# Trunk layer on one core: plain weight halves first, their sums in the halves' own places, and modulation rows in groups of 256 columns with tiles of their own

## The chip, the core and the metric

The kernel runs on one core of a Trainium2 chip. The metric is the device time of one execution in microseconds (us). Before the change it is 1999.14 us, the median of 3 runs (1997.41 to 2001.65).

## The reference, cut to what matters

One layer over 1056 tokens (1024 of a prompt, 32 of a second request with a condition vector of its own), model width 1024, all in float32:

```python
x = layer_norm(x)                                     # shared input norm
mod = silu(c) @ w_ada + b_ada                         # (9, 1024) for each of the two requests
f = (silu(mod1(x) @ w1) * (mod1(x) @ w3)) @ w2        # first feed-forward, width 2816
x = layer_norm(alpha * x + 0.5 * g1 * f)
m = mixer(mod2(x))                                    # RG-LRU group and gated spatial group
x = layer_norm(alpha * x + g2 * m)
f = (silu(mod3(x) @ v1) * (mod3(x) @ v3)) @ v2        # second feed-forward
x = layer_norm(alpha * x + 0.5 * g3 * f)
```

`modk(x)` is `x * (1 + scale_k) + shift_k`, and `g_k` is `1 + gate_k`. The nine rows of `mod` (three of shift, scale and gate each) come from one vector-matrix product with `w_ada`, 1024 x 9216.

## The kernel before

Activations lie transposed: 128 features to a partition block, 8 blocks, the tokens along the free axis in three chunks of 384, 384 and 288 columns (`CH`). A float32 product is made of three float32r matmuls: every operand is split into a high and a low part, and high*high, high*low and low*high are added in PSUM (`h_mm`, `p_mm`, `f_mm`, all through `mm`, L149). The split (`split`, L207 on ScalarE for the high part, L208 for the low one on VectorE, or on GpSimd where the caller says so) is made on the chip for weights and activations alike.

A feed-forward goes over 22 tiles of 128 hidden columns, in blocks of two (`BLOCKS`; the first and the last have three). For a tile, the H step makes the two products with `w1` and `w3`; for a block, the F step multiplies its gated tiles with `w2` and adds them into the residual (`add_gated`, L946 on VectorE).

From tile 3 on, the H step is `H_fast`: the two weight matrices are the rows of a 2 x 2 matrix of blocks (A11, A12 from `w1`, A21, A22 from `w3`, each 128 x 512 in memory, "halves" here), and the first two token chunks are the columns of another (B); seven products replace eight, in the manner of Strassen and Winograd. They need four sums of weight halves, S1 = A21 + A22, S2 = S1 - A11, S3 = A11 - A21, S4 = A12 - S2, made on GpSimd in `w_source` (L238, L239, L241, L243), and four sums of activation blocks, T1 to T4, made once for a feed-forward in `combs` and `comb_last` on VectorE (L789, L790). The third token chunk is multiplied in the plain way with the plain halves ("the sides"). PSUM has 8 banks, taken in turn by `ps`.

The order on TensorE is the order in which the code is written. A tile's eight weight halves are split in the order `PARTS` = A11, S2, A12, S1, S3, A22, S4, A21 into a ring of 8 tiles (`RING`) ahead of their use. Their raw form, 512 KB for `w1` and 512 KB for `w3` of a tile, is loaded by the SP queue (L202) into a ring of 5 tiles (`RAWS`), which also takes S1 and S2 (`wsum`) and the raw loads of `w_ada`. VectorE, ScalarE, GpSimd and SP get their order from a planner that simulates the program with times of its own; within an engine, instructions run strictly in that order, so one that waits holds up all behind it.

Two of the nine modulation rows are made at the start. The other seven (m = 2 to 8) are made during the first feed-forward by the generator `ada_rest`, which steps on as TensorE's planned time passes. For each half row of 512 columns it loads four tiles of 128 x 2 x 512 of `w_ada` (L698), accumulates 16 products with the condition vectors on VectorE (`acc`, L715 and L717), splits the sums, adds them over the partitions with four matmuls against a column of ones (`psm`), copies the two rows of the result to SBUF in two pieces (L732, into `s` tiles, the ring that the H step's intermediate results use too), writes them to DRAM (L733, on GpSimd's DMA queue), reads them back turned, so that the columns lie along partitions (L736, twice, same queue), and adds the bias on VectorE (`mod`, L738). Row 2, a gate, is needed by the first F step; the others later.

Of the kernel before, what the change touches and what calls it, by code (L numbers as in the profile page):

```python
# [12 lines left out]
F32 = mybir.dt.float32  # L13
# [38 lines left out]
PARTS = ["A11", "S2", "A12", "S1", "S3", "A22", "S4", "A21"]  # L52
RING, RAWS = 8, 5
# [68 lines left out]
class Core:  # L122
    def __init__(self, tc, ins, outs):
# [5 lines left out]
        self.n_s = 5  # L129
        self.ada_live = True  # L130
# [47 lines left out]
    def w_init(self):  # L178
        self.order = stream_order()
        self.raw_list = raw_order()  # L180
        self.raws = {}
        self.ws = {}
        self.sums = {}
        self.n_raw = self.n_split = self.n_rel = self.n_get = 0
        self.ring = [self.home(e) is None for e in self.order]
# [41 lines left out]
    def w_source(self, e):  # L227

        nm, t, h = e
# [4 lines left out]
        G = self.nc.gpsimd  # L234
        if h == "S2":
            x = self.wpool.tile([P, 1024], F32, tag="raw", name="wsum", bufs=RAWS)
            self.sums[nm, t] = x
            G.tensor_tensor(x[:, 0:512], a["A21"], a["A22"], ALU.add)  # L238
            G.tensor_tensor(x[:, 512:1024], x[:, 0:512], a["A11"], ALU.subtract)  # L239
        if h == "S3":  # L240
            G.tensor_tensor(a["A11"], a["A11"], a["A21"], ALU.subtract)  # L241
        if h == "S4":
            G.tensor_tensor(a["A12"], a["A12"], self.sums[nm, t][:, 512:1024], ALU.subtract)  # L243
        x = self.sums.get((nm, t))
        return {"S1": lambda: x[:, 0:512], "S2": lambda: x[:, 512:1024], "S3": lambda: a["A11"],
                "S4": lambda: a["A12"]}.get(h, lambda: a[h])()
# [25 lines left out]
    def w_rel(self, k=2):  # L272

        self.n_rel += k
        while self.n_split < len(self.order):
# [7 lines left out]
        need = {r for e in self.order[:n + 4] for r in raws_of(e)}  # L283
        open_ = {r for e in self.order[n:n + 16] for r in raws_of(e)} & set(self.raws)
        room = RAWS - self.ada_live - len(open_) - any(
            e[2] == "S4" and (e[0], e[1]) in self.sums for e in self.order[n:n + 8])
# [5 lines left out]
    def run(self):  # L292
# [51 lines left out]
        self.ffn(1, self.go(self.combs()), bg)  # L344
        self.drain(bg)
        self.ada_live = False
# [12 lines left out]
        self.n_s = 6  # L359
# [330 lines left out]
    def ada_rest(self):  # L690
# [4 lines left out]
        def raw(n):  # L695
            if n < 56 and n not in raws:
                r = self.wpool.tile([P, 2, 512], F32, tag="raw", name="raw", bufs=RAWS)
# [3 lines left out]
        raw(0)  # L701
        yield 1.0
        for m in (2, 3, 4, 5, 6, 7, 8):
            for h in range(2):
                acc = self.gpool.tile([P, 2, 512], F32, tag="acc", name="acc", bufs=1)
                for q in range(4):
                    n = ((m - 2) * 2 + h) * 4 + q
                    raw(n)
                    raw(n + 1)
                    r = raws.pop(n)  # L710
                    for kk in range(2):
                        k = 2 * q + kk
                        for v in range(2):
                            if k == 0:
                                V.tensor_scalar(acc[:, v, :], r[:, kk, :], self.cs[:, k, v:v + 1], None, ALU.mult)  # L715
                            else:
                                V.scalar_tensor_tensor(acc[:, v, :], r[:, kk, :], self.cs[:, k, v:v + 1],  # L717
                                                       acc[:, v, :], ALU.mult, ALU.add)
                    yield 2.5 if m == 2 else 7.0
                yield 5.0 if m == 2 else 9.0  # L720
                ps = self.ps("psm")
                for v in range(2):
                    t = [self.apool.tile([P, 512], F32R, tag="tot", name="acchl", bufs=self.ntot) for _ in range(2)]
                    self.split(t[0], t[1], acc[:, v, :])
# [862 lines left out]
```

## Time and profile before

| What | Value |
|---|---|
| median of 3 runs | 1999.14 us (1997.41 to 2001.65) |
| profiled execution | 2002.01 us, span 2000.3 us |
| mean granted TensorE clock | 0.971 |
| busy: TensorE, VectorE | 1876.9 us (94%), 1346.2 us (67%) |
| busy: ScalarE, GpSimd | 709.2 us (35%), 524.8 us (26%) |
| DMA | 140.16 MB, 70 GB/s mean |
| chain that ended last, largest share | TensorE 54% |

The stages in the span: start and the first H tile, with two modulation rows, to about 100 us; the rest of the first feed-forward to about 900 us, with the other seven rows until 773 us; the mixer to about 1300 us; the second feed-forward and the last norm to the end. The stage views give for each engine its busy time and, in brackets, its instructions; a matmul count in a stretch of equal kind of work is the measure of progress.

### The profile page before, as it was taken

How to read it: one execution, taken by the hardware profiler on the slowest of the kernel's cores; microseconds unless marked ns; L12 is line 12 of the kernel's file. 1: busy time of each engine (PE TensorE's matmuls, PEld its weight loads, DVE VectorE, ACT ScalarE, POOL GpSimd, SP SyncE). 2: the span in 40 equal slices, each digit the busy share in tenths (PEclk: the TensorE clock that was granted, in tenths of full speed). 3: DMA queues.
4: the chain of work that ended last, by engine and by line, in shares of the span. 5: the costliest groups of instructions: out<-in, count | busy, mean ns of one | idle time of the engine just before them, and what ended most of it. 6: DMA issues, size and time to landing. Idle time of an engine off the chain costs nothing.

```text
span 2000.3 us, 28452 instructions
## 1 busy us (share of the span) xinstructions
PE 1876.9 (94%) x11362; PEld 1819.9 (91%) x11362; DVE 1346.2 (67%) x2390; ACT 709.2 (35%) x1240; POOL 524.8 (26%) x428
## 2 busy tenths in 40 slices
PE   6979898899999898998999999999999999999996
PEld 3869898898998897998978999999999999999996
DVE  6889677687777685477397647695555545554567
ACT  5552222322322322325554434723222332223224
POOL 2213333333333433302200000023233323233310
PEclk8989899999999998999989999999999999999998
DMA  7331222222222220122201231001101111111102
GB/s 267 117 105 54 86 94 75 85 95 75 95 85 74 85 84 23 57 71 95 82 3 60 68 136 39 21 23 58 64 33 53 43 64 43 43 43 64 43 11 87
DMA packets 40949, 140.16 MB, mean 70 GB/s; under 512 B 6072, under 2 KB 8816, under 8 KB 40048
## 3 DMA queue, kind: packets, MB, share of 16 engines
q1 hardware_dynamic: 37104, 128.98, 18.9%
q10 hardware_dynamic: 1920, 9.24, 1.2%
q0 software_dynamic: 1792, 0.12, 0.4%
q8 instruction: 89, 1.46, 0.3%
q14 instruction: 44, 0.36, 0.1%
HBM read 129.53 MB, written 8.79 MB: 69 GB/s over the span
## 4 chain that ended last, share of the span: by engine, by line
PE 54%; DVE 5%; ACT 1%; issue 0%; POOL 0%; DMA 0%; POOLq 0%; DVEq 0%; ACTq 0%
PE ps L149 52%; PE psl L149 1%; PE psz L149 1%; DVE s L789 1%; PE psg L149 0%; DVE tot L952 0%; DVE xb L1065 0%; ACT t L543 0%; DVE t L1076 0%; DVE wh L208 0%; DVE xa L946 0%; DVE tx L208 0%; DVE xb L946 0%; ACT xh L550 0%; DVE s L790 0%
## 5 line engine op out<-in xcount | busy, mean ns | idle before, releaser
L149 PE MATMUL ps<-xh,wh 128*128 128x384 f32 (+1 forms) x3824 | 923.0, 324 | 45.1 <-DVE s L838 41.0
L149 PEld LDWEIGHTS ps<-xh,wh 128*128 128x128 f32 x3824 | 677.4, 192 | 55.6 <-DVE s L838 46.5
L149 PE MATMUL ps<-xl,wh 128*128 128x384 f32 (+1 forms) x1912 | 616.9, 323 | 3.3 <-DVE xl L553 3.2
L149 PE MATMUL ps<-g,wh 128*128 128x384 f32 (+1 forms) x2808 | 466.1, 325 | 13.0 <-DVE xa L946 4.7
L149 PEld LDWEIGHTS ps<-g,wh 128*128 128x128 f32 x2808 | 453.6, 189 | 19.6 <-DVE xa L946 6.7
L207 ACT ACTIVATE wh<-raw 128x512 fp32r<-128x512 f32 x376 | 234.7, 629 | 540.5 <-PE ps L149 517.1
L149 PEld LDWEIGHTS ps<-xl,wh 128*128 128x128 f32 x1912 | 367.4, 192 | 7.3 <-DVE xl L553 5.3
L208 DVE TENSOR_TENSOR wh<-raw,wh 128x512 fp32r<-128x512 f32 x283 | 207.2, 737 | 197.8 <-ACT wh L207 195.6
L208 POOL TENSOR_TENSOR wh<-raw,wh 128x512 fp32r<-128x512 f32 x93 | 129.3, 1392 | 417.0 <-ACT wh L207 416.9
L946 DVE SCALAR_TENSOR_TENSOR xb<-ps,gt,xb 128x384 f32<-128x384 f32 (+1 forms) x352 | 152.7, 488 | 102.6 <-PE ps L149 87.3
L717 DVE SCALAR_TENSOR_TENSOR acc<-raw,cs,acc 128x512 f32<-128x512 f32 x196 | 168.8, 897 | 6.5 <-DMA raw<-ada 6.3
L149 PE MATMUL ps<-tx,wh 128*128 128x384 f32 x912 | 167.3, 338 | 2.7 <-DVE s L838 2.6
L838 DVE TENSOR_TENSOR s<-s,ps 128x384 f32<-128x384 f32 x190 | 104.7, 551 | 87.4 <-PE ps L149 79.7
L149 PEld LDWEIGHTS ps<-tx,wh 128*128 128x128 f32 x912 | 158.9, 190 | 4.4 <-DVE s L838 3.6
L946 DVE SCALAR_TENSOR_TENSOR xa<-ps,gt,xa 128x384 f32<-128x384 f32 (+1 forms) x320 | 136.0, 481 | 23.5 <-PE ps L149 23.1
L208 POOL TENSOR_TENSOR wh<-wsum,wh 128x512 fp32r<-128x512 f32 x76 | 104.5, 1375 | 60.3 <-ACT wh L207 59.6
L207 ACT ACTIVATE g<-s 128x384 fp32r<-128x384 f32 (+1 forms) x126 | 62.4, 496 | 144.5 <-DVE s L679 144.0
L208 DVE TENSOR_TENSOR g<-s,g 128x384 fp32r<-128x384 f32 (+1 forms) x126 | 83.9, 666 | 39.4 <-ACT g L207 39.4
L238 POOL TENSOR_TENSOR wsum<-raw 128x512 f32<-128x512 f32 x38 | 57.8, 1522 | 142.4 <-DVE wh L208 86.0
L241 POOL TENSOR_TENSOR raw<-raw 128x512 f32<-128x512 f32 x38 | 53.3, 1403 | 148.1 <-DVE wh L208 101.5
L567 POOL TENSOR_TENSOR r<-r,half 128x3 f32<-128x3 f32 x8 | 7.4, 924 | 312.1 <-DVE r L566 312.1
L149 PE MATMUL ps<-T,wh 128*128 128x384 f32 x456 | 86.2, 337 | 0.0
(231 smaller groups left out, 1809.3 us busy)
## 6 DMA issues: line engine op xcount, KB each, us to landing
raw<-wst SPq DMA_DIRECT2D x156, 512.0 KB, 3.2
raw<-ada SPq DMA_DIRECT2D x64, 512.0 KB, 3.3
wnat<-ada SPq DMA_DIRECT2D x8, 512.0 KB, 9.9
xt<-x SPq DMA_DIRECT2D x7, 512.0 KB, 7.6
sp<-xa ACTq DMA_DIRECT2D x2, 1536.0 KB, 5.0
xb<-sp ACTq DMA_DIRECT2D x2, 1536.0 KB, 10.5
y<-xb SPq DMA_DIRECT2D x4, 768.0 KB, 3.2
sp<-xa ACTq DMA_DIRECT2D x1, 1152.0 KB, 4.1
```

The lines of the kernel that those rows point to most:

```text
L149: self.nc.tensor.matmul(out, a, b, start=start, stop=stop, skip_group_check=True)
L207: self.nc.scalar.activation(dst_h, src, AF.Copy)
L208: (e or self.nc.vector).tensor_tensor(dst_l, src, dst_h.bitcast(F32), ALU.subtract)
L238: G.tensor_tensor(x[:, 0:512], a["A21"], a["A22"], ALU.add)
L241: G.tensor_tensor(a["A11"], a["A11"], a["A21"], ALU.subtract)
L567: self.nc.gpsimd.tensor_tensor(out, out, self.half[:n, :w], ALU.pow)
L717: V.scalar_tensor_tensor(acc[:, v, :], r[:, kk, :], self.cs[:, k, v:v + 1], acc[:, v, :], ALU.mult, ALU.add)
L789: e.tensor_tensor(r, x[i][:, k, :].bitcast(F32), y[i][:, k, :].bitcast(F32), op)
L838: V.tensor_tensor(out, x, ps[:, :n], ALU.add)
L946: V.scalar_tensor_tensor(X[:, m, a + o:a + o + w], ps[:, o:o + w], self.gt[:, s, m, v:v + 1], X[:, m, a + o:a + o + w], ALU.mult, ALU.add)
```

## The change

Five things change.

- **Order of the halves.** `PARTS` becomes A11, A21, A12, A22, S2, S1, S3, S4, and `H_fast` is written in that order, with the sides put right behind the halves they use: A11, its side, A21's side, A12, its side, A22 (with T4), S2, S1, A22's side, S3, S4. The tile's last product is now S4's.
- **Sums in place.** A21 becomes S3, A22 becomes S2, A11 becomes S1 and A12 becomes S4, each in its own raw tile, with four GpSimd operations as before; `wsum` is gone. `RAWS` is 4, and raw tiles are asked for 12 halves ahead instead of 4 (4 in the first part of the mixer).
- **Modulation rows.** A unit is 256 columns: four loads of 128 x 2 x 256 (256 KB each), 32 accumulating operations of half the width for what took 16 before, and one row copy. Loads and row copies share a ring of their own, `ar`, of 2 tiles. The steps behind the sums (write, read back, bias) are written a step of the next unit's accumulation apart each, and the read-back and the bias come once for two units.
- **Activation sums of the first feed-forward.** T1 and T3 are made on GpSimd there (differences and low parts), with longer spacing; T2, T4 and the second feed-forward stay on VectorE.
- **F step.** With the block's last tile, the chunks 0, 2, 1 are taken over all of the group's output blocks instead of block by block. An `s` tile more (6) is there from the start.

```diff
-PARTS = ["A11", "S2", "A12", "S1", "S3", "A22", "S4", "A21"]
-RING, RAWS = 8, 5
+PARTS = ["A11", "A21", "A12", "A22", "S2", "S1", "S3", "S4"]
+RING, RAWS = 8, 4
...
-        if h == "S2":
-            x = self.wpool.tile([P, 1024], F32, tag="raw", name="wsum", bufs=RAWS)
-            self.sums[nm, t] = x
-            G.tensor_tensor(x[:, 0:512], a["A21"], a["A22"], ALU.add)
-            G.tensor_tensor(x[:, 512:1024], x[:, 0:512], a["A11"], ALU.subtract)
-        if h == "S3":
-            G.tensor_tensor(a["A11"], a["A11"], a["A21"], ALU.subtract)
-        if h == "S4":
-            G.tensor_tensor(a["A12"], a["A12"], self.sums[nm, t][:, 512:1024], ALU.subtract)
+        if h == "A22":
+            G.tensor_tensor(a["A21"], a["A11"], a["A21"], ALU.subtract)
+        if h == "S2":
+            G.tensor_tensor(a["A22"], a["A22"], a["A21"], ALU.subtract)
+            G.tensor_tensor(a["A11"], a["A11"], a["A22"], ALU.add)
+        if h == "S1":
+            G.tensor_tensor(a["A12"], a["A12"], a["A22"], ALU.subtract)
...
-        need = {r for e in self.order[:n + 4] for r in raws_of(e)}
+        need = {r for e in self.order[:n + self.ahead] for r in raws_of(e)}
...
-                r = self.wpool.tile([P, 2, 512], F32, tag="raw", name="raw", bufs=RAWS)
+                r = self.gpool.tile([P, 2, 256], F32, tag="ar", name="araw", bufs=2)
                 nc.sync.dma_start(r, self.i["ada1"][n])
...
+            row = self.gpool.tile([P, 512], F32, tag="ar", name="row", bufs=2)[0:2, 0:256]
+            nc.scalar.activation(row, ps[0:2, 0:256], AF.Copy)
+            return row
...
+        def after(m, h, hl):
+
+            row = sums(m, h, hl)
+            yield
+            out(m, h, row)
+            if h % 2 == 0:
+                return
+            yield
+            back(m, h)
+            yield
+            use(m, h)
...
+            for q in range(4):
+                n = i * 4 + q
+                raw(n)
+                r = raws.pop(n)
+                for kk in range(2):
...
+                    yield w
+                    if kk == 0 and q and pre:
+                        next(pre, None)
+                raw(n + 1)
...
-        self.ffn(1, self.go(self.combs()), bg)
+        self.ffn(1, self.go(self.combs(nc.gpsimd)), bg)
...
-                for js in (range(J - 1), [J - 1]):
-                    for m in ms:
-                        for j in js:
-                            for c in range(3) if j == 0 else (0, 2, 1):
-                                self.f_mm(ps[m][c], ws[j], gs[j], PIECES[c], 4 * h + m, j == 0, j == J - 1)
+                for j in range(J):
+                    for m, c in ([(m, c) for c in (0, 2, 1) for m in ms] if j == J - 1 else
+                                 [(m, c) for m in ms for c in range(3)]):
+                        self.f_mm(ps[m][c], ws[j], gs[j], PIECES[c], 4 * h + m, j == 0, j == J - 1)
```

How the planned order moves is seen in three places, all in the first fast tiles of the first feed-forward. First VectorE around the bias addition `mod` of row 3's first half. Before (`raw` here is a tile of `w_ada`, `s<-s,ps` takes a product out of PSUM):

```order
L838 TENSOR_TENSOR s<-s,ps 128x384
L717 SCALAR_TENSOR_TENSOR acc<-raw,cs,acc 128x512 x6
L208 TENSOR_TENSOR wh<-raw,wh 128x512
L717 SCALAR_TENSOR_TENSOR acc<-raw,cs,acc 128x512
L738 TENSOR_TENSOR mod<-mod,vec 128x8
L717 SCALAR_TENSOR_TENSOR acc<-raw,cs,acc 128x512
L838 TENSOR_TENSOR s<-s,ps 128x384 x3
```

and the same addition in the changed program, which stands in the next tile:

```order
L208 TENSOR_TENSOR wh<-raw,wh 128x512
L762 SCALAR_TENSOR_TENSOR acc<-araw,cs,acc 128x256 x4
L673 TENSOR_TENSOR s<-s,ps 128x288
L762 SCALAR_TENSOR_TENSOR acc<-araw,cs,acc 128x256 x2
L208 TENSOR_TENSOR g<-s,g 128x288
L762 SCALAR_TENSOR_TENSOR acc<-araw,cs,acc 128x256 x2
L871 TENSOR_TENSOR s<-s,ps 128x384
L722 TENSOR_TENSOR mod<-mod,vec 128x8
L208 TENSOR_TENSOR acchl<-acc,acchl 128x256
```

The addition comes later against the tile's products: before, three of their PSUM reads stand behind it, now one stands right ahead of it, and the next unit's sums are finished around it.

Second GpSimd, which makes the weight sums and issues the rows' DMAs. Before, around row 4's second half:

```order
L238 TENSOR_TENSOR wsum<-raw 128x512
L239 TENSOR_TENSOR wsum<-wsum,raw 128x512
L241 TENSOR_TENSOR raw<-raw 128x512
L208 TENSOR_TENSOR wh<-wsum,wh 128x512
L733 DMA mrow_1_3282<-s 2x256 x2
L736 DMA mod<-mrow_1_3282 128x4x1 x2
L243 TENSOR_TENSOR raw<-raw,wsum 128x512
L208 TENSOR_TENSOR wh<-wsum,wh 128x512
```

and in the changed program, around the second half of row 3:

```order
L208 TENSOR_TENSOR wh<-raw,wh 128x512 x2
L710 DMA mrow_2053<-row 2x256
L208 TENSOR_TENSOR wh<-raw,wh 128x512 x2
L237 TENSOR_TENSOR raw<-raw 128x512
L710 DMA mrow_2053<-row 2x256
L716 DMA mod<-mrow_2053 128x4x1
L239 TENSOR_TENSOR raw<-raw 128x512
L716 DMA mod<-mrow_2053 128x4x1
```

A half row's two writes were issued together, right ahead of the read-back; now the first is issued a unit earlier, and only the second stands right ahead of it.

Third the SP queue, which issues the loads. Before, in the first fast tiles:

```order
L698 DMA raw<-ada 128x1024
L202 DMA raw<-wst 128x1024 x2
L698 DMA raw<-ada 128x1024 x2
L202 DMA raw<-wst 128x1024
L698 DMA raw<-ada 128x1024
```

and now:

```order
L692 DMA araw<-ada 128x512 x4
L202 DMA raw<-wst 128x1024 x4
L692 DMA araw<-ada 128x512 x6
L202 DMA raw<-wst 128x1024 x2
L692 DMA araw<-ada 128x512 x4
```

Weights (`wst`) are asked for in groups of two to four, further ahead; between them stand four to six of the smaller loads.

More of the change, by code (lines that the diff above doesn't have):

```diff
@@ L695, in raw @@
         def raw(n):
[L696 to L697 removed]
+            if n < 112 and n not in raws:
+                r = self.gpool.tile([P, 2, 256], F32, tag="ar", name="araw", bufs=2)
                 nc.sync.dma_start(r, self.i["ada1"][n])
                 raws[n] = r
[L701 to L721, printed above, removed]
[L722 to L738 removed]
@@ new lines, in ada_rest, with sums, out @@
+        rows, pre = {}, None
+        def sums(m, h, hl):
+            ps = self.ps("psm")
+            for v in range(2):
+                for q in range(2):
+                    self.mm(ps[0:2, 0:256], self.one_r[:, v, :], hl[v][:, q], v + q == 0, v + q == 2)
+            row = self.gpool.tile([P, 512], F32, tag="ar", name="row", bufs=2)[0:2, 0:256]
+            nc.scalar.activation(row, ps[0:2, 0:256], AF.Copy)
+            return row
+        def out(m, h, row):
+            if h == 0:
+                rows[m] = self.dram.tile([2, 1024], F32, name=f"mrow{m}")
+            nc.gpsimd.dma_start(rows[m][:, h * 256:(h + 1) * 256], row)
@@ new lines, in back, with use @@
+        def back(m, h):
+            f0 = 2 * h - 2
+            with nc.allow_non_contiguous_dma(reason="a kilobyte of modulation, turned"):
+                for v in range(2):
+                    nc.gpsimd.dma_start(self.mod[:, m, f0:f0 + 4, v],
+                                        rows[m][v, f0 * P:(f0 + 4) * P].rearrange("(f p) -> p f", p=P))
+        def use(m, h):
+            f0 = 2 * h - 2
+            mod = self.mod[:, m, f0:f0 + 4, :]
+            self.late = V.tensor_tensor(mod, mod, b_ada[:, m, f0:f0 + 4].unsqueeze(2).to_broadcast([P, 4, 2]), ALU.add)
+            if h < 3:
+                return
@@ L842, in H_fast @@
         self.p_mm(pa, a11, B11, True, False)
[L843 to L851 removed]
+        y0 = self.new_s()
+        S.activation(y0, pa[:, :n], AF.Copy)
+        if not later:
+            third(0, 0, a11)
+        self.w_rel(k)
+        a21 = get("A21")
@@ L859, in H_fast @@
+        w = get("S2")
+        self.p_mm(pb, w, self.T2, True, False)
+        y1 = self.new_s()
+        add(y1, y0, pb)
+        self.w_rel(1)
         w = get("S1")
         self.p_mm(pc, w, self.T1, True, False)
-        self.w_rel(1)
+        z1 = self.new_s()
+        S.activation(z1, pc[:, :n], AF.Copy)
+        g = None
+        if not later:
+            g = self.gs[t] = self.new_g(self.g_tag(t))
+            third(1, 1, a22)
+            self.glu_end(g, 2, y2, sides[1][:, :CH[2][1]])
@@ L1456, in mix @@
         self.apool, self.es_a2 = self.pool("a2", side="left")
+        self.ahead = 12
         self.xacc = []
```

149 lines of the change are left out of this document (71 added, 78 removed).

## The prediction

> **What bounds the kernel now.** I read the stage windows first: stretch, length, then busy us of TensorE (PE) with its matmuls in brackets, its weight loads, VectorE (DVE), ScalarE, GpSimd (POOL), granted clock, DMA.
>
> ```profile
> 100.00:200.00 100.00, 83.19 (x483) 79.73 (x483) 90.19 (x167) 39.69 (x79) 23.68 (x19) 0.93 0.24 80
> 200.00:750.00 550.00, 504.72 (x3001) 492.33 (x3000) 411.24 (x689) 154.21 (x292) 198.55 (x162) 0.95 0.26 85
> 750.00:800.00 50.00, 40.44 (x226) 39.03 (x225) 29.78 (x74) 10.18 (x19) 15.89 (x14) 0.90 0.08 24
> ...
> 1350.00:1900.00 550.00, 550.00 (x3443) 548.60 (x3442) 294.13 (x548) 162.57 (x291) 184.88 (x138) 1.00 0.15 50
> ```
>
> The last row, second feed-forward, is TensorE without a gap: 3443/550 = 6.26 matmuls a us. At that rate the same kind of work in 200 to 750 would take 3001/6.26 = 479 us, so 71 us are lost there; likewise 23 us in 100 to 200 and 14 us in 750 to 800: 108 us in all. TensorE sets the time, and only the first feed-forward has anything to give. Who holds it up stands in the waits of 160 to 800 us (total, times, longest):
>
> ```profile
> PE ps L149 <- DVE s L838: 43.6, 12, 8.5
> PE ps L149 <- DVE xa L946: 4.7, 3, 2.4
> ...
> DVE mod L738 <- DMA mod<-mrow: 45.7, 12, 4.9
> DVE wh L208 <- ACT wh L207: 36.8, 32, 3.2
> ...
> DVE acc L717 <- DMA raw<-ada: 6.3, 4, 2.8
> DVE s L838 <- DMA mrow<-s: 6.0, 2, 3.8
> ```
>
> TensorE waits 12 times for VectorE to empty a PSUM bank (L838); VectorE waits 12 times in the bias addition for the read-back of a modulation row. That these are one thing shows the order of time:
>
> ```profile
> 208.01 0.74 DVE L717 SCALAR_TENSOR_TENSOR acc<-raw,cs,acc 128x512 f32<-128x512 f32 x1
> 212.61 1.89 DVE L738 TENSOR_TENSOR mod<-mod,vec 128x8 f32<-128x8 f32 x1 [3.86 <-DMA mod<-mrow]
> ...
> 215.09 1.79 DVE L838 TENSOR_TENSOR s<-s,ps 128x384 f32<-128x384 f32 x3
> ...
> 216.27 0.69 PE L149 MATMUL ps<-xh,wh 128*128 128x384 f32 x1 [8.54 <-DVE s L838]
> ...
> 217.07 0.84 PE L149 MATMUL ps<-xh,wh 128*128 128x384 f32 x2
> ...
> 225.14 0.51 PE L149 MATMUL ps<-xh,wh 128*128 128x384 f32 x2
> ```
>
> VectorE sits 3.86 us in front of `mod`, the L838 operations queue behind it, TensorE stands 8.54 us. Then a pair of matmuls takes 0.84 us where it takes 0.51 later: some 6 us at a reduced clock after the stall. In 200 to 750, 45 us are idle time and the other 26 us mostly such slow matmuls.
>
> **The change part by part.** *The row's round trip.* At the last half row the sums, the two writes, the two read-backs and the addition start at
>
> ```profile
> 760.89 0.62 PE L149 MATMUL psm<-acchl,one_r 128*2 128x512 f32 x2
> ...
> 762.34 0.54 POOL L733 DMA_DIRECT2D mrow<-s  x1 [8.42 <-ACT s L732]
> ...
> 764.65 0.55 POOL L733 DMA_DIRECT2D mrow<-s  x1 [0.46 <-ACT s L732]
> 766.86 0.78 POOL L736 DMA_DIRECT2D mod<-mrow  x1 [1.66 <-issue]
> 769.77 0.77 POOL L736 DMA_DIRECT2D mod<-mrow  x1 [2.13 <-issue]
> ...
> 772.52 0.17 DVE L738 TENSOR_TENSOR mod<-mod,vec 128x8 f32<-128x8 f32 x1 [3.24 <-DMA mod<-mrow]
> ```
>
> That is 11.0 us from the end of the sums (761.5). With one row copy and one write behind the last sums instead of two, 2.3 us fall out (764.65 against 762.34): about 8.7 us, an estimate. Counting matmuls in the planned orders at 6.26 a us, the addition's neighbours on VectorE belong 4 to 8 us behind the sums before, 7 to 14 us behind them in nine of twelve cases now. So the addition comes when its data has landed or up to 2 us short of it. Of the 45.7 us I leave 6. The 6.0 us on `mrow<-s` go whole, since a row no longer sits in an `s` tile.
>
> *A new wait in its place.* The row now sits in one of two slots that the loads of `w_ada` also use. Of a unit's four loads the third cannot start before the second is used up, the fourth not before the row is written out.
>
> ```profile
> raw<-ada SPq DMA_DIRECT2D x64, 512.0 KB, 3.3
> ...
> raw<-lruw SPq DMA_DIRECT2D x4, 128.0 KB, 2.0
> ...
> mrow<-s POOLq DMA_DIRECT2D x28, 2.0 KB, 2.5
> ```
>
> A 256 KB load lies between 2.0 and 3.3 us; I take 2.7. The fourth lands 0.8 (row copy, until 762.34 above) + 2.5 + 2.7 = 6.0 us behind the sums, and the order wants it 4.5 to 8 us behind them: 1 us of wait on average. The third has 2 us of other VectorE work ahead of it: 0.5 us. At 22 units in the stretch this is 33 us (bounds 0 and, with 3.3 us loads and no cover, 22 x 3 = 66), against 51 us that go (45.7 - 6, 6.0, and most of the 6.3). Behind a waiting `acc` stand the tile's PSUM reads, behind a waiting load on SP up to four weight loads.
>
> *Half-width accumulation.* Twice as many operations.
>
> ```profile
> L717 DVE SCALAR_TENSOR_TENSOR acc<-raw,cs,acc 128x512 f32<-128x512 f32 x154 | 136.5, 921 | 6.3 <-DMA raw<-ada 6.3
> L717 DVE SCALAR_TENSOR_TENSOR acc<-raw,cs,acc x196: 732/744/1953, 93.6 to 736.5; 128x512 f32<-128x512 f32 x196
> L715 DVE TENSOR_SCALAR acc<-raw,cs 128x512 f32<-128x512 f32 x20 | 10.8, 579 | 0.3
> L946 DVE SCALAR_TENSOR_TENSOR xa<-ps,gt,xa 128x384 f32<-128x384 f32 x112 | 66.5, 607 | 14.9 <-PE ps L149 14.5
> L946 DVE SCALAR_TENSOR_TENSOR xa<-ps,gt,xa 128x256 f32<-128x256 f32 x56 | 26.4, 471 | 0.0
> ```
>
> An undisturbed 512-wide one takes 744 ns; 256 columns less at L946's slope, (607-471)/128 ns each, leave 472. Successive ones overlap by 35 ns (136.5/154 against 921). So 348 x 0.437 = 152 us. The disturbed ones (mean 921, longest 1953) add 177 ns x 154 = 27 us today. If that is tied to GpSimd's operations, whose number stays, it remains 27; if to VectorE's, it becomes 348 x 0.177 = 62. The longest exceeds the median by 1.21 us, about one GpSimd operation (L241 below, 1.44 us), so I take 27: 152 + 27 = 179 us for today's 147, and VectorE's busy time in the stretch 411 + 32 = 443 us (bounds 411, if cost halves with width, and 478).
>
> The Trainium skill ("SBUF — State Buffer", section "Who interferes with whom") says that a VectorE instruction with two SBUF inputs and a GpSimd one that reads SBUF exclude each other for a whole instruction. By it the blocked time follows GpSimd's operations, 27 us, and the longest L717 agrees; by the other reading VectorE would need 35 us more here, and the rival that makes it the bound would weigh more. The same rule speaks against the first block's edit: by it each of the operations moved to GpSimd there can block VectorE for its own length.
>
> *What this stretch comes to.* VectorE then needs 443 + 6 + 33 = 482 us, TensorE 479. Two engines of equal length that pass work to and fro will not reach 479, but the waits are shorter than the 3.9 us that make today's stalls. I take 25 of the 71 us as still lost (bounds 5 and 65): a gain of 46.
>
> *First block.* Eight of T1's and T3's steps move to GpSimd.
>
> ```profile
> PE psm L149 <- ACT acchl L207: 10.4, 2, 6.2
> L789 DVE TENSOR_TENSOR s<-xh,xh 128x384 f32<-128x384 f32 x16 | 11.0, 684 | 0.0
> L790 DVE TENSOR_TENSOR s<-s 128x384 f32<-128x384 f32 x32 | 18.3, 572 | 0.1
> L241 POOL TENSOR_TENSOR raw<-raw 128x512 f32<-128x512 f32 x15 | 21.6, 1440 | 15.9 <-DVE wh L208 13.2 <-issue 2.5
> ```
>
> VectorE loses 8 x (2 x 0.68 + 2 x 0.57) = 20 us of work, where it is 90% busy and TensorE waits for its sums; it gains 32 operations and the disturbance by 32 GpSimd ones of about 1.1 us (L241's, scaled to 384). Gate row 2 must still be back before the first F step. Of 23 us lost I count 4 as gained (bounds -6 and +15).
>
> *End.* At 750 to 800 row copies and softplus stand in front of TensorE; row 8 now ends a tile before the last block: 10 of 14 us (bounds 5 and 14).
>
> *Order of halves, last product.* Behind S4 follows F at once; the side products that covered its chain are gone.
>
> ```profile
> L838 DVE TENSOR_TENSOR s<-s,ps 128x384 f32<-128x384 f32 x75 | 41.1, 549 | 18.6 <-PE ps L149 15.7 <-DMA mrow<-s 2.2
> L679 DVE TENSOR_TENSOR s<-s 128x384 f32<-128x384 f32 x30 | 22.8, 762 | 2.6 <-ACT s L876 2.4
> L876 ACT ACTIVATE s<-s 128x384 f32<-128x384 f32 x15 | 7.8, 520 | 4.0 <-DVE s L838 3.9
> L207 ACT ACTIVATE g<-s 128x384 fp32r<-128x384 f32 x30 | 15.7, 522 | 51.1 <-DVE s L679 50.8
> L208 DVE TENSOR_TENSOR g<-s,g 128x384 fp32r<-128x384 f32 x30 | 23.4, 779 | 9.4 <-ACT g L207 9.4
> ```
>
> The chain takes 3.1 us; its cover is 18 matmuls of the other tile (2.9 us) and 12 of chunks 0 and 2 (1.9 us). With VectorE 53% busy in the second feed-forward I charge 1 us (bounds 0 and 9, 1 us at each of nine blocks). Sums in place, 4 raw tiles and loading 12 halves ahead I cost at nothing: the ring of 8 split halves, a tile of 132 matmuls or 21 us, hides them; without it a load's 3.3 us would show. The row sums keep their columns (56 matmuls of 512, 112 of 256).
>
> Sum: 46 + 10 + 4 - 1 = 59 us. The profiled execution took 2002.0 us, so 1943; it lies 2.9 us above the median of the runs, so 1940 for that.
>
> **The rivals.** *The new waits take over.* If each unit's third and fourth load cost 3 us together, VectorE needs 443 + 6 + 66 = 515 us, TensorE gains about 35 in the long stretch less the 20 for the handshake: 15 + 10 + 4 - 1 = 28, 1971 us. For it: two slots for three users. Against it: a late VectorE meets loads that have landed.
>
> *The full gain.* Small waits vanish in eight PSUM banks: 66 + 14 + 10 = 90, 1909 us. Against it VectorE's 443 of 479.
>
> *The additions still wait.* The planner has moved them ahead of where they are written; if the chain is nearer 12 us than 9, most of the 45.7 stays: only the end's 10 us, 1989.
>
> *Slower: VectorE becomes the bound of 200 to 750.* If an accumulating operation costs near as much at half the width, 0.82 us or more in place of 0.44, then 264 (the rest of its work) + 348 x 0.82 = 549 us is as much as the stretch lasts now; with 40 us of its waits for ScalarE on top it would be 2030 us. For it: 90% busy in the first block already. Against it: L946 gets 0.14 us shorter with 128 columns.
>
> **How the numbers follow.** Forecast 0.52 (own range 1920 to 1960), new waits 0.21, full gain 0.13, additions 0.06, slower 0.08. 0.2% or 4 us is about what a measurement of this kernel can tell from no change. Faster 0.89, within 0.02, slower 0.09. The range 1905 to 1988 leaves out the slower case and the ends of two others.
>
> **What would show it.** In the changed profile: the wait of `mod` on its read-back below 10 us; TensorE's waits for `s` below 20 us; 200 to 700 near 3250 matmuls per 550 us and a clock of 0.97 or more; `acc` operations of 0.45 to 0.55 us; waits of `acc` on its loads of some 30 us; the second feed-forward unchanged. I am wrong if `acc` stays above 0.7 us, or if TensorE's stalls stay as many and only change the name behind them.

## The result, and the profile after

The changed kernel takes 2032.5 us (median of 4 runs, 2028.7 to 2036.4), the kernel before beside it 1999.8: a ratio of 1.0164, 95% interval 1.0142 to 1.0187. It is 1.6% slower, where 1940 us were forecast. The profiled execution has a span of 2029.9 us against 2000.3.

The stage windows of the changed kernel, with the columns of the prediction's first fence:

```profile
200.00:750.00 550.00, 503.52 (x3008) 493.59 (x3009) 437.57 (x855) 159.99 (x319) 187.29 (x154) 0.95 0.27 80
...
1350.00:1900.00 550.00, 542.25 (x3374) 538.62 (x3373) 309.30 (x549) 160.69 (x298) 185.00 (x134) 1.00 0.15 49
```

The long stretch does 3008 matmuls in 550 us instead of 3001, so none of the 46 us came. The second feed-forward, which was to stay as it was, falls from 3443 to 3374.

Where the time went is seen best between the same F steps of the two traces. Each feed-forward has ten; the stages run from the start to the first F, from there to the ninth, on to the end of the first feed-forward, through the mixer to the first F of the second, from there to its ninth, and to the end:

| us | to first F | to ninth F | end of first | mixer | second | rest |
|---|---|---|---|---|---|---|
| before | 152.3 | 621.6 | 132.2 | 405.0 | 535.3 | 154.0 |
| changed | 157.1 | 621.6 | 134.3 | 412.2 | 543.4 | 161.3 |
| difference | +4.8 | 0.0 | +2.1 | +7.2 | +8.1 | +7.3 |

The waits of 200 to 750 us of the changed kernel (total, times, longest):

```profile
DVE acc L762 <- DMA araw<-ada: 25.0, 18, 2.3
DVE wh L208 <- ACT wh L207: 23.4, 21, 4.1
PE ps L150 <- ACT s L878: 22.0, 8, 5.5
...
ACT wh L207 <- POOL raw L239: 12.3, 7, 5.4
...
DVE mod L722 <- DMA mod<-mrow: 10.0, 4, 3.1
PE ps L150 <- DVE g L208: 9.5, 8, 2.7
...
PE ps L150 <- DVE s L871: 9.1, 4, 3.8
...
PE ps L150 <- ACT g L207: 7.2, 5, 2.6
...
DVE acc L760 <- DMA araw<-ada: 5.5, 2, 2.9
```

and of the kernel before, in the same stretch, VectorE's (over 200 to 750 us, not 160 to 800 as in the prediction) and one of ScalarE's:

```profile
DVE mod L738 <- DMA mod<-mrow: 42.5, 11, 4.9
DVE wh L208 <- ACT wh L207: 31.0, 28, 3.2
ACT wh L207 <- POOL wsum L239: 18.8, 4, 5.8
...
DVE s L838 <- PE ps L149: 15.7, 20, 2.0
...
DVE xa L946 <- PE ps L149: 14.5, 14, 1.5
...
DVE g L208 <- ACT g L207: 11.5, 18, 1.3
...
DVE acchl L208 <- ACT acchl L207: 8.9, 7, 2.8
```

The read-back wait fell from 42.5 to 10.0 us and the loads' wait came, 30.5 us, both near what was forecast (6 and 33). TensorE's stalls changed their name: the first bank of a tile is now read late by a copy on ScalarE (L878), and F waits for the gates. VectorE waited for TensorE only some 30 us of the 550 even before (15.7 + 14.5); the rest it worked, or waited for others.

One stall behind L878, on ScalarE and TensorE at a tile boundary of the changed kernel:

```profile
602.29 0.52 ACT L207 ACTIVATE g<-s 128x384 fp32r<-128x384 f32 x1 [2.84 <-DVE s L673]
602.76 0.52 ACT L922 ACTIVATE s<-s 128x384 f32<-128x384 f32 x1
...
603.91 0.52 ACT L207 ACTIVATE g<-s 128x384 fp32r<-128x384 f32 x1 [0.63 <-DVE s L673]
604.34 0.47 ACT L878 ACTIVATE s<-ps 128x384 f32<-128x384 f32 x1
...
604.87 0.69 PE L150 MATMUL ps<-xh,wh 128*128 128x384 f32 x1 [4.10 <-ACT s L878]
```

ScalarE keeps its order. The copy for the new tile stands behind the gates of the old one, which wait for VectorE; with S4 as the last product these two meet.

A block end of the second feed-forward, where no modulation row is made:

```profile
1468.77 3.23 PE L150 MATMUL ps<-g,wh 128*128 128x384 f32 x19
...
1471.02 1.47 POOL L239 TENSOR_TENSOR raw<-raw 128x512 f32<-128x512 f32 x1 [3.37 <-DVE wh L208]
1471.26 3.20 DVE L208 TENSOR_TENSOR g<-s,g 128x384 fp32r<-128x384 f32 x2
...
1472.57 1.48 POOL L240 TENSOR_TENSOR raw<-raw 128x512 f32<-128x512 f32 x1
1472.96 1.28 PE L150 MATMUL ps<-g,wh 128*128 128x384 f32 x6 [0.95 <-DVE g L208]
```

Two `g` operations, 0.55 us each when alone, take 3.20 us while GpSimd makes the sums in place, and TensorE stands 0.95 us, 19 matmuls into F. This repeats at eight block ends.

### The profile page after: what moved, and what is told of

The parts are those of the page before. It is cut to its first block, busy times and chain, and to the rows that moved or that the text cites. A ratio compares the mean times of both kernels' runs of the same rounds, so it can differ in the third digit from the quotient of the medians.

```text
span 2029.9 us, 29097 instructions
## 1 busy us (share of the span) xinstructions
PE 1886.5 (93%) x11418; PEld 1831.6 (90%) x11418; DVE 1402.2 (69%) x2610; ACT 725.3 (36%) x1306; POOL 567.3 (28%) x460
## 4 chain that ended last, share of the span: by engine, by line
PE 48%; DVE 7%; ACT 2%; issue 1%; POOL 1%; POOLq 0%; DVEq 0%; ACTq 0%; DMA 0%
PE ps L150 46%; PE psl L150 1%; DVE wh L208 1%; DVE g L208 1%; DVE s L673 1%; DVE s L871 1%; ACT t L537 1%; PE psg L150 0%; PE psz L150 0%; DVE tot L986 0%; ACT wh L207 0%; DVE s L913 0%; DVE xb L1098 0%; ACT xh L544 0%; DVE t L1109 0%
## 5 line engine op out<-in xcount | busy, mean ns | idle before, releaser
L150 PE MATMUL ps<-xh,wh 128*128 128x384 f32 (+1 forms) x3824 | 935.1, 324 | 34.1 <-ACT s L878 32.9
L150 PE MATMUL ps<-g,wh 128*128 128x384 f32 (+1 forms) x2808 | 477.6, 329 | 29.7 <-DVE g L208 18.3
L207 ACT ACTIVATE wh<-raw 128x512 fp32r<-128x512 f32 x452 | 279.9, 628 | 577.5 <-PE ps L150 514.0
L208 POOL TENSOR_TENSOR wh<-raw,wh 128x512 fp32r<-128x512 f32 x169 | 243.1, 1454 | 280.0 <-ACT wh L207 279.6
L762 DVE SCALAR_TENSOR_TENSOR acc<-araw,cs,acc 128x256 f32<-128x256 f32 x392 | 227.6, 626 | 37.3 <-DMA araw<-ada 37.1
L237 POOL TENSOR_TENSOR raw<-raw 128x512 f32<-128x512 f32 x38 | 52.1, 1370 | 340.7 <-DVE wh L208 320.5
L980 DVE SCALAR_TENSOR_TENSOR xa<-ps,gt,xa 128x384 f32<-128x384 f32 (+2 forms) x320 | 137.3, 482 | 10.1 <-PE ps L150 9.9
L871 DVE TENSOR_TENSOR s<-s,ps 128x384 f32<-128x384 f32 x152 | 81.9, 549 | 85.3 <-PE ps L150 84.3
L208 DVE TENSOR_TENSOR g<-s,g 128x384 fp32r<-128x384 f32 (+1 forms) x126 | 99.4, 796 | 38.1 <-ACT g L207 36.3
L239 POOL TENSOR_TENSOR raw<-raw 128x512 f32<-128x512 f32 x38 | 56.1, 1477 | 193.3 <-DVE wh L208 193.3
L668 ACT ACTIVATE s<-ps 128x384 f32<-128x384 f32 (+1 forms) x94 | 42.1, 451 | 108.0 <-PE ps L150 107.7
```

The lines of the kernel that those rows point to most:

```text
L150: self.nc.tensor.matmul(out, a, b, start=start, stop=stop, skip_group_check=True)
L207: self.nc.scalar.activation(dst_h, src, AF.Copy)
L208: (e or self.nc.vector).tensor_tensor(dst_l, src, dst_h.bitcast(F32), ALU.subtract)
L237: G.tensor_tensor(a["A21"], a["A11"], a["A21"], ALU.subtract)
L239: G.tensor_tensor(a["A22"], a["A22"], a["A21"], ALU.subtract)
L668: self.nc.scalar.activation(s, x[:, :n], AF.Silu)
```

## The experiments

Two theories, each with its part. **A**: the new order with sums in place costs at the tile and block ends, in both feed-forwards; A1 says for want of the cover behind S4, A2 because GpSimd's sums come in a burst that blocks VectorE. **B**: in the first feed-forward VectorE's total is what counts, its work and its waits for all but TensorE; the row change put as much in as it took out.

The stages of all runs, from their profiled executions, with the median of the timed runs. The last two columns are for 200 to 750 us: the time that 3000 matmuls took, and VectorE's own time for them (busy plus waits not for TensorE; before: (411.2 + 104.8) x 3000/3001 = 516).

| kernel | median | to first F | to ninth F | end of first | mixer | second | rest | 3000 matmuls | VectorE's own |
|---|---|---|---|---|---|---|---|---|---|
| before | 1999.8 | 152.3 | 621.6 | 132.2 | 405.0 | 535.3 | 154.0 | 550 | 516 |
| changed | 2032.5 | 157.1 | 621.6 | 134.3 | 412.2 | 543.4 | 161.3 | 549 | 511 |
| rows alone | 2001.0 | 149.5 | 611.4 | 136.6 | 410.6 | 535.4 | 155.1 | 536 | 501 |
| all but rows | 2044.8 | 167.4 | 626.1 | 136.9 | 404.4 | 543.6 | 162.8 | 554 | 531 |
| three slots | 2031.0 | 154.1 | 623.1 | 134.6 | 412.7 | 543.3 | 161.3 | 549 | 514 |
| late bias | 1978.5 | 151.5 | 600.6 | 131.9 | 404.4 | 535.3 | 154.0 | 531 | 490 |
| late bias, row | 1952.2 | 147.7 | 580.4 | 128.8 | 404.3 | 535.3 | 153.9 | 517 | 479 |
| the same, half width | 1976.8 | 153.9 | 599.3 | 128.3 | 404.3 | 535.2 | 153.9 | 532 | 504 |
| 4 ahead | 2027.1 | 157.7 | 615.9 | 134.6 | 412.7 | 542.3 | 162.3 | 544 | 507 |
| own sums | 1988.8 | 156.6 | 589.1 | 130.4 | 413.2 | 535.4 | 159.5 | 517 | 486 |
| side last | 2009.4 | 157.5 | 609.8 | 137.8 | 411.9 | 532.8 | 160.7 | 539 | 501 |
| T1, T3 on VectorE | 2019.8 | 148.6 | 615.7 | 134.5 | 412.1 | 543.4 | 161.3 | 545 | 512 |
| order and rows only | 1985.8 | 149.6 | 584.6 | 140.1 | 413.4 | 538.4 | 159.5 | 513 | 487 |
| order, late wide rows | 1961.3 | 148.1 | 575.2 | 132.8 | 406.4 | 538.0 | 157.7 | 515 | 480 |

A row's stages come from one execution, and executions of one kernel lie 2 to 10 us apart, so differences of 2 or 3 us in the first feed-forward say little. In every row the time of 3000 matmuls lies 24 to 42 us above VectorE's own time. That difference is, by the way it is worked out, little else than VectorE's waits for TensorE. It is a pattern over fourteen traces; the edits below are what shows causes.

### All but the rows, and the rows alone

Into the changed kernel the old `ada_rest` with its 512 columns (and raw tiles and `s` tiles to fit):

```diff
-                r = self.gpool.tile([P, 2, 256], F32, tag="ar", name="araw", bufs=2)
+                r = self.wpool.tile([P, 2, 512], F32, tag="raw", name="raw", bufs=RAWS)
...
-            row = self.gpool.tile([P, 512], F32, tag="ar", name="row", bufs=2)[0:2, 0:256]
+                    row = self.new_s()[0:2, 0:256]
```

> The changed kernel with the modulation rows made as before (512 columns, row copies in the s ring, one raw tile of five kept for w_ada; s ring of 5 in the first feed-forward); new are only the order of the halves, the sums in place, the F order and the first block's sums on GpSimd. Theory A (the order of the halves with sums in place costs at every block end, in both feed-forwards; the row change by itself is a gain): the second feed-forward keeps its 16 us of loss, and the first one, with the old 45 us of waits for the read-back on top of the dearer block ends, is 15 to 25 us longer than in the kernel before: 2035 to 2050 us. Theory B (VectorE's total is what counts in the first feed-forward: the row change swapped its waits for work and took back what it gave; the halves cost only what the second feed-forward and the mixer show): 2018 to 2028 us.

Into the kernel before the new `ada_rest`, the reverse of this diff:

> The kernel before with the modulation rows of the changed one (units of 256 columns, ring of two for loads and row copies, spread round trip) and nothing else new; four raw tiles, all for the weights, as many as the weights had. Theory A: the old block ends keep their cover, the second feed-forward is as before, and the first gains 15 to 30 us: 1970 to 1985 us. Theory B: the row change gains nothing by itself, since 26 us of VectorE work and 24 us of waits for loads stand in the place of the waits that go: 1992 to 2006 us.

Measured: 2044.8 us (ratio 1.0231, 1.0215 to 1.0246) and 2001.0 (1.0007, 0.9995 to 1.0019). Without the rows the change costs 45 us, which is A's number, but in part by luck: the first F starts 15 us later, a place of which A says nothing (the sums on GpSimd, below). The rows alone are worth nothing, B's number. The rows alone, 200 to 750 us (windows, then waits, then the group of `acc`: count, busy us, mean ns, idle before):

```profile
200.00:750.00 550.00, 508.86 (x3078) 499.33 (x3077) 446.13 (x863) 161.48 (x314) 184.34 (x158) 0.95 0.27 83
```

```profile
PE ps L149 <- DVE s L877: 35.6, 11, 8.2
...
DVE acc L768 <- DMA araw<-ada: 25.7, 17, 3.3
...
DVE mod L728 <- DMA mod<-mrow: 4.6, 1, 4.6
```

```profile
L768 DVE SCALAR_TENSOR_TENSOR acc<-araw,cs,acc 128x256 f32<-128x256 f32 x288 | 162.8, 612 | 25.7 <-DMA araw<-ada 25.7
```

The `mod` wait loses 38 us; VectorE works 35 us more (446.1 against 411.2) and waits 19 us more for loads (25.7 against 6.3). TensorE still waits 35.6 us for L877, the former L838. The 10 us that the fast tiles gain are given back at the end of the first feed-forward (+4.4) and in the mixer (+5.6), and of the mixer B says nothing. All kernels with narrow rows have a mixer of 411 to 413 us, all with wide rows one of 404 to 406. But no row is made in the mixer, and each of the kernels with narrow rows also has four raw tiles where the others have five. No run parts these two, so the mixer's loss may be the smaller ring's. In the mixer, from about 1000 us on, the changed kernel's trace shows seven waits of TensorE, 8.3 us together, and the one before four, 4.5 us.

### Three slots in the ring

```diff
-                r = self.gpool.tile([P, 2, 256], F32, tag="ar", name="araw", bufs=2)
+                r = self.gpool.tile([P, 2, 256], F32, tag="ar", name="araw", bufs=3)
...
-        self.n_s = 6
+        self.n_s = 5
```

> The changed kernel with three slots in the ring that the loads of w_ada and the row copies share instead of two (room from one s tile less in the first feed-forward). The waits of acc for its loads, 37 us in the profile, fall below 10. Theory B (VectorE's total decides): most of these come off the first feed-forward, 2005 to 2015 us. Theory A (the block ends decide, the load waits lie in VectorE's slack): at most 8 us, 2024 to 2032.

Measured: 2031.0 us (1.0157, 1.0142 to 1.0172), A's number. For `acc`, all operations of the tile, what ended VectorE's and ScalarE's idle time before them, in this kernel:

```profile
  DVE acc L763: 55.8, 25
  DMA araw<-ada: 11.9, 11
```

The loads' wait fell to 11.9 us, from 42.6 in the changed kernel, and nothing was gained: 3000 matmuls still take 549 us. VectorE's other waits rose instead (`wh <- ACT` from 23.4 to 39.8 us, `mod` from 10.0 to 19.7). With one `s` tile less this is not a pure test, but it gives theory B no support for the loads' part. It shows too that such waits can stand in for one another: a wait that is taken away is not always time gained.

### The late bias, and the row in another ring

The kernel before, with the bias addition and what hangs on it moved into a function `use` that is called in the next half row:

```diff
+                    if q == 2 and pend:
+                        use(*pend)
+                        pend = None
```

> The kernel before with one edit: the bias addition of a half row is written into the next half row's accumulation, behind its third load, so that on VectorE it stands some 20 to 35 places behind the split of the sums instead of 5 to 17. Widths, rings and halves stay. It tests the first term of the prediction by itself: the waits of mod for its read-back, 46 us, should fall below 12. Theory B: VectorE then has 35 us less to do and to wait in the first feed-forward and nothing in their place, so most of it is gained: 1965 to 1980 us. If the stalls of TensorE only change their name (theory A's view, the stall goes to the next late thing): 1985 to 2000.

Measured: 1978.5 us (0.9896, 0.9879 to 0.9912), in B's range. Its waits in 200 to 750:

```profile
DVE mod L703 <- DMA mod<-mrow: 8.6, 3, 4.4
ACT s L750 <- DMA mrow<-s: 8.1, 3, 3.7
...
DVE s L849 <- DMA mrow<-s: 6.0, 2, 3.8
```

So the prediction's first term was sound: 34 us of `mod` wait are gone, and with nothing put in their place 21 us are gained between the first and the ninth F. The next thing is the row copy that sits in an `s` tile until it is written out. With that mended too:

```diff
-                for q in range(2):
-                    row = self.new_s()[0:2, 0:256]
-                    nc.scalar.activation(row, ps[0:2, q * 256:(q + 1) * 256], AF.Copy)
-                    nc.gpsimd.dma_start(d[:, q * 256:(q + 1) * 256], row)
+                row = self.apool.tile([P, 512], F32, tag="tot", name="row", bufs=self.ntot)[0:2, :]
+                nc.scalar.activation(row, ps[0:2, :], AF.Copy)
+                nc.gpsimd.dma_start(d, row)
```

> The kernel before with the late bias addition and one edit more: the row of the sums is copied in one piece into the ring of the split sums (tot) instead of in two pieces into the s ring, and written in one transfer. In the late-bias run VectorE and ScalarE still wait 20 us in 200 to 750 for the write of a row to free its s tile, and two of TensorE's stalls of 6.5 us stand behind that. If such waits decide, another 10 to 18 us go: 1960 to 1969 us. If TensorE's stalls go to the next late thing: 1972 to 1980 us.

Measured: 1952.2 us (0.9766, 0.9747 to 0.9784), 26 us below the run before and more than expected (1960 to 1969). The edit moves the row and also makes one copy and one write of two; no run parts these. This is the best version: it beats both kernels with two edits to the one before.

### The width by itself

The best version, each `acc` operation made as two of 256 columns:

```diff
                         for v in range(2):
+                            for c in (slice(0, 256), slice(256, 512)):
```

> The fastest kernel so far (old halves, wide rows, late bias, row in the ring of the split sums; 1952 us) with one edit: each accumulating operation of 512 columns is made as two of 256. Loads, rows, rings and waits stay as they are, so only the width is new. The prediction put VectorE's extra work in 200 to 750 us at 32 us (two of 0.437 us for one of 0.886 with disturbance shared) and thought it would lie in slack. If VectorE's work in that stretch is on the path (theory B), 15 to 30 us come back: 1967 to 1982 us. If it lies in slack: 1950 to 1958 us, and the narrow rows' handicap comes from their waits for loads and for slots.

Measured: 1976.8 us (0.9885, 0.9862 to 0.9908): 24.6 us come back. The `acc` groups of 200 to 750 us, wide and then half width, and the windows of both:

```profile
L732 DVE SCALAR_TENSOR_TENSOR acc<-raw,cs,acc 128x512 f32<-128x512 f32 x149 | 132.0, 920 | 3.7 <-DMA raw<-ada 3.5
```

```profile
L733 DVE SCALAR_TENSOR_TENSOR acc<-raw,cs,acc 128x256 f32<-128x256 f32 x308 | 172.3, 614 | 4.6 <-DMA raw<-ada 4.6
```

```profile
200.00:750.00 550.00, 526.84 (x3189) 515.19 (x3189) 435.03 (x752) 163.05 (x296) 207.18 (x160) 0.98 0.27 86
```

```profile
200.00:750.00 550.00, 516.73 (x3104) 504.15 (x3103) 460.21 (x881) 161.59 (x293) 197.83 (x158) 0.97 0.27 87
```

One wide operation costs 132.0/149 = 0.886 us, two narrow ones 2 x 172.3/308 = 1.119. Over the 196 operations of the program that is 0.233 x 196 = 46 us of work more, and the kernel is 24.6 us longer: about half of the extra work is on the path, which is theory B's point, and the other half is hidden. VectorE is busy 25 us more in the stretch and TensorE does 85 matmuls less.

### Sums in place, and loads further ahead

The changed kernel with S1 and S2 made in a tile of their own from the four, and loads asked for 4 halves ahead:

```diff
-            G.tensor_tensor(a["A22"], a["A22"], a["A21"], ALU.subtract)
-            G.tensor_tensor(a["A11"], a["A11"], a["A22"], ALU.add)
+            x = self.wpool.tile([P, 1024], F32, tag="raw", name="wsum", bufs=RAWS)
+            G.tensor_tensor(x[:, 0:512], a["A21"], a["A22"], ALU.add)
+            G.tensor_tensor(x[:, 512:1024], x[:, 0:512], a["A11"], ALU.subtract)
...
-        self.ahead = 12
+        self.ahead = 4
```

> The changed kernel with S1 and S2 in a tile of their own again (of the four raw tiles; loads asked for 4 halves ahead), the order of the halves and everything else as changed. A sum no longer has to wait until the plain half whose place it takes has been split, so the four GpSimd sums don't come in a row at the block's end. Theory A2: VectorE's excess over its undisturbed durations in the second feed-forward, 41 us in the changed kernel and 23 before, falls back towards 23, and the second feed-forward and the last stretch lose 0 to 4 us instead of 15: 2012 to 2022 us. Theory A1 (missing cover alone): 1 us stays at each block end: 2028 to 2034 us.

Measured: 1988.8 us (0.9942, 0.9927 to 0.9958), far below either number. To part the two edits, the changed kernel with only `ahead` at 4:

> The changed kernel with raw tiles asked for 4 halves ahead instead of 12 (and no raw tile held back in the mixer), the sums still made in place. The run with sums in tiles of their own had both undone and took 1989 us instead of 2032; this one tells which of the two it was. If the sums in place are the cause (a sum waits until VectorE or GpSimd has split the half it overwrites): 2024 to 2036 us, with TensorE's 1.0 us waits at the block ends of the second feed-forward. If the early loads are the cause (they stand in front of the loads of w_ada on SP's queue): 1986 to 2002 us.

Measured: 2027.1 us (1.0130, 1.0104 to 1.0156). So the early loads cost 5 us, and the sums in place 2027.1 - 1988.8 = 38. With S1 and S2 in a tile of their own the other two sums move as well: S3 and S4 are made right ahead of their own splits, as in the kernel before, and not with A22 and S1. So the place and the burst are undone together, and no run parts them. In the profiled executions 27 us of the difference lie between the first and the ninth F and 7 in the second feed-forward. Waits of ScalarE, TensorE and GpSimd in 200 to 750 us, sums in place (4 ahead), then own sums (L884 is L878 there):

```profile
POOL raw L239 <- DVE wh L208: 61.5, 12, 7.0
...
PE ps L150 <- ACT s L878: 20.9, 7, 5.5
...
ACT wh L207 <- POOL raw L240: 9.6, 6, 4.1
...
PE ps L150 <- DVE g L208: 8.8, 8, 2.7
ACT wh L207 <- POOL raw L239: 8.7, 8, 4.0
```

```profile
POOL wsum L240 <- DVE wh L209: 64.6, 7, 12.0
...
PE ps L150 <- ACT s L884: 9.1, 4, 2.9
...
PE ps L150 <- DVE g L209: 2.4, 5, 0.5
...
ACT wh L208 <- POOL wh L209: 1.6, 1, 1.6
```

A sum in place must wait until the half that it overwrites has been split (L239 makes S2 in A22's place), and that split waits for a place in the ring of halves. S1 and S2 with a tile of their own don't overwrite a half, but GpSimd waits for VectorE's splits there too (L240). What goes is ScalarE's waiting for the sums; TensorE's for the copy halves, and its 8 to 9 us each for the gates' high parts and for VectorE stay. Waits of ScalarE for a sum are not new, though: the kernel before had 18.8 us of them. Which of these waits carries the 38 us is not shown.

The second feed-forward is back at 535.4 us. The last stretch is not: it takes 159.5 us against 154.0, and 157.7 or more in every kernel with the new order; the cause is open. Over the 19 fast tiles of the second feed-forward, the time from VectorE's read of S4's product to the end of the low part of that gate is on average 3.8 us before, 4.7 in the changed kernel and 3.4 with own sums, and GpSimd is busy for 1.4, 2.9 and 1.0 us of it (worked out from the three traces). What VectorE's operations took beyond the lower quartile of their kind comes to some 23, 41 and 30 us in 1350 to 1900.

### The side product last, and T1 and T3 on VectorE

```diff
-            third(1, 1, a22)
-            self.glu_end(g, 2, y2, sides[1][:, :CH[2][1]])
...
         self.glu_end(g, 1, y1, z1)
+        if not later:
+            third(1, 1, a22)
+            self.glu_end(g, 2, y2, sides[1][:, :CH[2][1]])
```

> The changed kernel with the side product of A22 put behind the tile's last product S4 again (12 matmuls of 288 columns, 1.6 us, between S4 and F). In the changed kernel TensorE waits 1.0 us at every block end of the second feed-forward, 18 matmuls into F, for the low part of chunk 0's gate, and 3 us at the last block. Theory A1 (the cover is what is missing): the 1.0 us go at each of eight block ends, as do most of the 19 us of such waits at F in the first feed-forward: 2008 to 2018 us. Theory A2 (four GpSimd sums in a row block VectorE at the block's end whatever stands behind S4): the wait only moves to chunk 2's gate, whose chain now starts 3.6 us later: 2024 to 2033 us.

Measured: 2009.4 us (1.0038, 1.0023 to 1.0054), A1's range: 1.6 us of TensorE work between S4 and F take the waits away although the sums stay in place. In 200 to 750 us TensorE's wait for the copy on ScalarE falls from 22.0 to 10.7 us, and its wait for VectorE's L871 rises from 9.1 to 21.7. The windows row of this kernel shows TensorE without a gap again:

```profile
1350.00:1900.00 550.00, 550.00 (x3450) 550.00 (x3449) 298.99 (x552) 168.93 (x313) 191.05 (x139) 1.00 0.15 50
```

So A1 and A2 are two halves of one thing: a chain made longer by the burst, and no cover left for it. Either mends the second feed-forward up to its ninth F.

```diff
-        self.ffn(1, self.go(self.combs(nc.gpsimd)), bg)
+        self.ffn(1, self.go(self.combs(nc.vector)), bg)
```

> The changed kernel with T1 and T3 of the first feed-forward back on VectorE. Start to the first F step took 152 us before, 157 in the changed kernel, 149.5 with the new rows alone and 167 with the new halves alone. If the GpSimd sums are what makes the start longer (16 GpSimd operations a sum tile there, which block VectorE's two-input operations), the first F step now begins near 150 us and the whole is 2022 to 2027 us. If the order of the halves is what costs there, it begins at 157 or later and the whole stays at 2029 to 2036 us. The rest of the program should not move by either.

Measured: 2019.8 us (1.0105, 1.0086 to 1.0125). The first F starts at 148.6 instead of 157.1, as expected for the sums on GpSimd being at fault. The whole lies 2 us below that range; the 6 us between the first and the ninth F were not expected.

### What is left of the change

> The changed kernel with three parts undone together: sums in tiles of their own (4 ahead), T1 and T3 of the first feed-forward on VectorE, A22's side product behind S4. Left of the change are the order with plain halves first, the F order and the rows of 256 columns. One by one these gave -43, -12 and -23 us. If they act at different places, start to first F step falls to 149 us, the idle time at F in the first feed-forward (12 us with own sums) falls below 4, and the whole is 1960 to 1972 us. If the side product and the sums mended the same wait (the block ends), only the start is added: 1973 to 1980 us.

Measured: 1985.8 us (0.9926, 0.9903 to 0.9950), outside both. Start and fast tiles gain as hoped (149.6, 584.6), but the end of the first feed-forward takes 140.1 us, with one stall of 8.9 us, and the second one loses 0.4 us a block again. The parts don't add: -38, -5, -23 and -13 one by one, -47 together.

> The same as the run before it in this list (order of plain halves first, own sums, T1 and T3 on VectorE, A22's side product last), but with the modulation rows of the kernel before, 512 columns wide, with the late bias addition and the row in the ring of the split sums. Against the kernel with these rows and the old order (1952 us) it tells what the order of the halves is worth by itself. If the order is worth nothing: 1945 to 1960 us. If narrow rows are better with it than wide ones, it lies above the run before it in this list.

Measured: 1961.3 us (0.9809, 0.9787 to 0.9830), 1 us above the range. Wide late rows are 24 us better than narrow ones with this order too. Against the best version with the old order, 1952.2, the new one gains 5 us in the fast tiles and loses 13 elsewhere (stages).

## Why the prediction was wrong

- **The cause of the stalls**, `mod` waiting for its read-back in front of the tile's PSUM reads: right. Taken away alone it gave 21 us, and 48 with the row out of the `s` ring and its two copies made one.
- **Round trip, 6 us left of 45.7**: right in kind; 13.2 us are left in the same 160 to 800 us, 10.0 of them in the long stretch. **New wait, 33 us**: right in size, 30.5; lowering it, with one `s` tile less, gave nothing.
- **Half-width accumulation, 179 us for today's 147**: nearly. The mean share of an operation is 164.8/285 = 0.578 us where 0.514 was put:

```profile
L762 DVE SCALAR_TENSOR_TENSOR acc<-araw,cs,acc 128x256 f32<-128x256 f32 x285 | 164.8, 624 | 25.2 <-DMA araw<-ada 25.0
```

  The disturbance is 164.8 - 285 x 0.437 = 40 us, or 49 for the 348 operations of the forecast, between the 27 and the 62 that were weighed.
- **"VectorE then needs 482 us, TensorE 479 ... 25 of the 71 us as still lost"**: this step failed. It set work, the `mod` wait and the loads' wait against TensorE, and left out VectorE's waits for ScalarE (31.0 + 11.5 + 8.9 = 51 us before). With them VectorE's own time was already 516 of 550 us, and by the prediction's own terms 65 us came in (32 and 33) for 51 that went. A gain of 46 could not follow. The runs showed in its place: the rows alone gained nothing (2001.0 us), the `mod` wait taken away with nothing put in its place gained 21, and half width by itself cost 25. The sum of waits is no forecast either, since in the run with three slots other waits rose as one fell.
- **First block, 4 gained**: failed, it lost 5; with T1 and T3 on VectorE the first F starts 8.5 us earlier.
- **End, 10 gained**: the stall at the ninth F did go, but the row work itself ended later, and the next block paid. The first number of the last pair is when the first, the second when the last of the bias additions starts, before and after:

```profile
L738 DVE TENSOR_TENSOR mod<-mod,vec x14: 166/246/1891, 134.5 to 772.5; 128x8 f32<-128x8 f32 x14
```

```profile
L722 DVE TENSOR_TENSOR mod<-mod,vec x14: 150/167/1021, 139.6 to 830.4; 128x8 f32<-128x8 f32 x14
```

  That row 8 ends a tile before the last block was read off the planned order; on the chip the ninth F ended at 802 us and the last addition came at 830, inside the last block.
- **Last product, 1 us (bounds 0 and 9)**: mis-sized. The mechanism was named, but the chain of 3.1 us was summed from the means of the kernel before, where GpSimd's sums come less in a burst, and charged in the second feed-forward only. With the side product last again the kernel is 23 us shorter; in the profiled executions 11 us of that lie in the second feed-forward and 12 between the first and the ninth F, while the end of the first loses 3.5.
- **"Sums in place, 4 raw tiles and loading 12 halves ahead I cost at nothing"**: the dearest miss, 38 + 5 us, the 38 with the time at which S3 and S4 are made. The ring of halves was named as cover for the loads. It covers no sum that must wait for a split out of the same ring.
- **The mixer** had no term and lost 7 us. They go with the narrow rows and as much with four raw tiles in place of five, which the prediction put at nothing; the cause is open.

The rival on the slower side gave 2030, but its condition, 0.82 us an operation, was not met, and 23 us of the loss lie behind the first feed-forward, where no `acc` runs. Its premise, that VectorE's work decides the long stretch, is borne out in part: about half of the added work came back as time.

## What to carry to other kernels

Before a wait is taken from an engine, add up its busy time and all its waits that are not for the engine that sets the time; if that already fills the stretch, a wait is worth what it holds only if nothing is put in its place. Here moving one addition and one small tile gave 2.3%, while a change that mended the same two waits, narrowed the operations and added waits for loads gave nothing by itself. Making a sum in place of its operand saves a tile and adds a wait for the operand's last reader: ask when that reader runs, and what the delayed work then lands on.

## What the runs showed of the hardware

A VectorE operation can be kept out over several GpSimd operations in a row, and the trace counts all of it as busy. In the changed kernel:

```profile
674.41 6.18 DVE L762 SCALAR_TENSOR_TENSOR acc<-araw,cs,acc 128x256 f32<-128x256 f32 x2
674.88 1.29 POOL L240 TENSOR_TENSOR raw<-raw 128x512 f32<-128x512 f32 x1
676.11 1.30 POOL L242 TENSOR_TENSOR raw<-raw 128x512 f32<-128x512 f32 x1
...
677.37 2.54 POOL L208 TENSOR_TENSOR wh<-raw,wh 128x512 fp32r<-128x512 f32 x2
```

```profile
L762 DVE SCALAR_TENSOR_TENSOR acc<-araw,cs,acc x392: 464/478/5787, 42.8 to 812.5; 128x256 f32<-128x256 f32 x196
```

The longest `acc` takes 5.79 us where the median is 0.48, and four GpSimd operations run meanwhile without a gap between them. Two more, at 374 and at 755 us, take 4.36 and 4.38 us over three. The prediction took the longest disturbance to be one GpSimd operation.

The Trainium skill ("SBUF — State Buffer", "Who interferes with whom") says that the engine that issues first has the shared ports for its whole instruction. This trace does not settle who came first: the long `acc` starts 0.47 us ahead of the first of the four by its record, and ends 0.30 us behind the last. What it shows is that the wait lasted for four instructions. At the block end shown above it lasted for one each time: the two `g` operations take 1.64 and 1.63 us, and each ends 0.4 us behind one GpSimd sum. What decides between the two is not shown.
